# Moving the first GLU pair ahead of three heads of v, the layer norm beside the last pairs, and one low half to DMA

## The chip, the core and the metric

The kernel runs on one core of a Trainium2 chip. The core has TensorE (PE, matrix products; PEld is its weight load), VectorE (DVE), ScalarE (ACT) and GpSimd (POOL), which work side by side, each through its own instructions in order. SyncE (SP) starts most DMA transfers, POOL those that accumulate into their destination. The metric is the time of the program on the device in microseconds: the median of the runs.

## The reference

One layer with two token mixers that share one input projection; x is 1024 tokens by 1024 channels, in float32:

```
h = rmsnorm(x, norm_g)
q, k, v, o, i, f, z_a, glu_in, z_b, ga, gb = split(h @ w_in)
q, k = silu(causal conv of 4 taps over q, k)
hm  = mLSTM(q, k, v, i, f), then RMS norm per head          # 4 heads of 256
y_a = (sigmoid(o) * hm * silu(z_a)) @ w_pa
u   = glu_in[:1024] * sigmoid(glu_in[1024:])
u   = causal conv of 31 taps per channel (u)
u   = silu(layernorm(u) over channels) * silu(z_b)
y_b = u @ w_pb
out = rmsnorm(x + (sigmoid(ga)*y_a + sigmoid(gb)*y_b) @ w_out)
```

## The kernel before, in words

**Products.** Each float32 operand is a high and a low part, and a product is three matmuls (high by high, high by low, low by high). `split` (L102, L103) makes the high part with ScalarE and the low part with VectorE.

**Stages.** First h is made and transposed into `hb`, beside head 0 of v. Then follow three `v_job`s (heads 1 to 3, each of 8 token tiles with 24 matmuls of 128x256; L312 copies four tiles at a time), the mLSTM's gates (`gates`) and `sums`, which forms the sums of blocks of h that Winograd's form of Strassen's scheme needs and keeps them in `ext`. After that come 36 `quad` jobs, called pairs here: each makes two groups of 128 output channels for all tokens out of seven products (X, Z, W banks of PSUM) of twelve 128x512 matmuls. `quad` copies banks with ScalarE (L412, L415, L418), combines with VectorE (L422, L426, L430), and `emit` applies the pair's function. After the pairs come the mLSTM in chunks of 256 tokens together with the projection y_b, then y_a and the output projection.

**Preparation.** `prep(n + 1)` runs beside job n (`run_job`): it splits the weight blocks a11 and a12 (tag "a"), forms the four sums s1 to s4 on VectorE (L198 to L203), splits them (tags "t" and "s") and a22 (tag "b"). For "t" and "s" the low half is a negated copy on ScalarE (L189) to which a DMA of POOL's queue adds the source (L190, `lo…t`, `lo…s`). For "a" and "b" VectorE subtracts (L103). The halves of one pair are `hi…a`, `lo…a` and so on with the job's number.

**Order.** The jobs are gb0 ga0 q0 k0 o0 za0 mb0 ma0, gb1 ga1 and so on, and last zb0 to zb3; numbers 4 to 39. gb and ga are the two sides of the GLU. `glu_job` (ga) leaves two tiles u, and each goes through the 31-tap convolution on VectorE (L498 once, L500 30 times) with a low priority, so that a scheduler places its steps between the other work. There is one accumulator tile `acc`; the finished tile is stored to c_dram by SP and added into s_dram (s1_dram, the sum over channel tiles) by a DMA of POOL (L505). An engine's instructions go in the order that the scheduler set, whatever is ready.

**Layer norm.** `layer_norm` runs beside the last two pairs ahead of zb0: the sum over channels by matmuls with ones (`token_stat`, `tstat`), a transpose (`trow`) and a trip through mu_dram to broadcast it; then eight centred tiles `ct` (`centred`: load, subtract), squared on ScalarE (L585) and added into `sv` by DMAs of POOL (L586); a second statistic, and rstd broadcast into `sv`. `zb_job` loads and centres each tile again, multiplies by `sv` (L599), takes the SiLU (L600), and its pair multiplies SiLU(z_b) by it (L453) and stores to u_dram.

Of the kernel before, what the change touches and what calls it, by code (L numbers as in the profile page):

```python
# [9 lines left out]
F32 = mybir.dt.float32  # L10
# [28 lines left out]
DMA_LOW = True  # L39
# [3 lines left out]
def kernel(ctx: ExitStack, tc: tile.TileContext, x, norm_g, w_in, b_if, conv_qk_w, conv_qk_b,  # L43
# [22 lines left out]
    def ms(name, shape=None):  # L66
# [4 lines left out]
    c_dram, q_dram, k_dram, g_dram, u_dram, oa_dram, sga_dram, sgb_dram, m1_dram = (  # L71
        dram(n, [KT, P, S]) for n in ("c_dram", "q_dram", "k_dram", "g_dram", "u_dram", "oa_dram", "sga_dram", "sgb_dram", "m1_dram"))
# [99 lines left out]
    def prep(n):  # L172
# [28 lines left out]
        s1, s2 = pair("t", sm[0], DMA_LOW)  # L201
# [3 lines left out]
        s3, s4 = pair("s", sm[1], DMA_LOW)  # L205
# [318 lines left out]
    for h in range(H):
        jobs.append(dict(kind="v", h=h, name="v", fn=lambda n, h=h: v_job(n, h)))
    rest = []
    for h in range(H):
        rest.append(("q", lambda n, h=h: qk_job(n, h, 0), Q0, h))
        rest.append(("k", lambda n, h=h: qk_job(n, h, 1), K0, h))
        rest.append(("o", lambda n, h=h: act_job(n, AF.Sigmoid, keep="gate"), O0, h))  # L530
        rest.append(("za", lambda n, h=h: act_job(n, AF.Silu, store=lambda j, h=h: g_dram[2 * h + j],
                                                 by=lambda j: state["gate"][j]), ZA0, h))
        rest.append(("mb", lambda n, i=h: act_job(n, AF.Sigmoid, store=lambda j, i=i: sgb_dram[2 * i + j]), MB0, h))
        rest.append(("ma", lambda n, i=h: act_job(n, AF.Sigmoid, store=lambda j, i=i: sga_dram[2 * i + j]), MA0, h))
    for i in range(4):
        add(f"gb{i}", lambda n: act_job(n, AF.Sigmoid, keep="sg"), GB0_, i)
        add(f"ga{i}", lambda n, i=i: glu_job(n, 2 * i), GA0_, i)
        for name, fn, base, h in rest[6 * i:6 * i + 6]:
            add(f"{name}{h}", fn, base, h)
    first_zb = len(jobs)  # L540
    for i in range(4):
        add(f"zb{i}", lambda n, i=i: zb_job(n, i), ZB0, i)
# [18 lines left out]
    def centred(c, n):  # L561
        ct = state["lnp"].tile([P, S], F32, tag="ct", name=f"ct{n}_{c}", bufs=2)
# [4 lines left out]
    def layer_norm():  # L567

        lnp = state["lnp"]
        mu = lnp.tile([P, S], F32, name="mu")  # L570
        sv = lnp.tile([P, S], F32, name="sv")
        state["mu"], state["rstd"] = mu, sv
        s1 = lnp.tile([P, S], F32, tag="ct", name="s1", bufs=2)
        nc.sync.dma_start(s1, s1_dram)
        ps, st = token_stat(s1, 0)
        nc.vector.tensor_scalar(st, ps, 1.0 / D, None, op0=ALU.mult)
        yield
        to_row(st, 0, mu)
        yield
        for c in range(KT):  # L580
# [6 lines left out]
            yield  # L587
# [462 lines left out]
```

## Time and profile before

| | us |
|---|---|
| runs, median of 3 (range) | 1343.44 (1343.11 to 1345.21) |
| the profiled execution | 1342.88 |
| its span | 1341.1 |
| TensorE busy | 1219.2 |
| VectorE busy | 947.3 |
| ScalarE busy | 624.4 |
| POOL busy | 121.7 |

The profile shows one execution. Its span is from the first instruction to the last; the time of the run has 1.8 us around it. An engine's idle time stands in the row of the instruction that ended it, with what released that instruction. Matmuls are pipelined, so that the starts of successive matmuls are the measure of their pace.

### The profile page before, as it was taken

Reading aid. Unit: us, or ns where it says so; the run is one execution under the profiler, and the core shown is the slowest. Engines: PE = TensorE matmul, PEld = TensorE weight load, DVE = VectorE, ACT = ScalarE, POOL = GpSimd, SP = SyncE. Lnnn points to the kernel's source line nnn. Section 1 sums busy time; section 2 is a strip of 40 time slices with the busy share of each in tenths; the row PEclk is TensorE's granted clock in tenths of the full one; section 3 lists DMA queues with packets and bytes.
Section 4 is the critical chain, followed back from the end, with each engine's and each line's share of the span. In section 5 each row is a group of like instructions: output and inputs, shape, how many; then the busy total and the mean of one; then the engine's idle time right before and its main releaser. Section 6 shows DMA issues by size and latency. Waiting matters only on the chain. (4 is left out here: it accounts for less than half of the span.)

```text
span 1341.1 us, 16597 instructions
## 1 busy us (share of the span) xinstructions
PE 1219.2 (91%) x6204; PEld 1025.1 (76%) x6204; DVE 947.3 (71%) x1250; ACT 624.4 (47%) x916; POOL 121.7 (9%) x229
## 2 busy tenths in 40 slices
PE   8999999999999999989999998255898999899997
PEld 7998878878787787877788786144787887588997
DVE  6882499798998979989798983247886763344433
ACT  6343456544564546644475453236745531222224
POOL 2100100101101010101001011100111110000002
PEclk9999999999999999999999898666899999899999
DMA  7224455766557566576566676748886544453403
GB/s 260 77 64 110 98 138 141 185 145 141 126 141 185 129 142 161 120 190 136 132 173 128 164 168 161 176 129 277 247 263 196 172 155 149 160 171 126 173 17 126
DMA packets 165022, 206.33 MB, mean 154 GB/s; under 512 B 9553, under 2 KB 134857, under 8 KB 164942
## 3 DMA queue, kind: packets, MB, share of 16 engines
q1 hardware_dynamic: 152558, 160.19, 38.1%
q0 software_dynamic: 12384, 45.09, 18.2%
q8 instruction: 48, 0.79, 0.2%
q14 instruction: 32, 0.26, 0.1%
HBM read 113.48 MB, written 50.36 MB: 122 GB/s over the span
## 5 line engine op out<-in xcount | busy, mean ns | idle before, releaser
L500 DVE SCALAR_TENSOR_TENSOR acc<-u,dww,acc 128x1024 f32<-128x1024 f32 x240 | 307.4, 1281 | 3.5
L112 PE MATMUL v<-hi,hb 128*128 128x256 f32 (+1 forms) x512 | 95.2, 289 | 2.5 <-ACT hb L102 2.0
L112 PE MATMUL ya<-oa,whi 128*128 128x512 f32 x256 | 86.4, 414 | 8.5 <-ACT oa L102 4.6
L112 PE MATMUL out<-whi,mrg 128*128 128x256 f32 x512 | 92.3, 283 | 0.0
L112 PE MATMUL yb<-u,whi 128*128 128x512 f32 x256 | 84.7, 407 | 2.0 <-ACT u L102 1.5
L112 PEld LDWEIGHTS v<-hi,hb 128*128 128x128 f32 x512 | 80.0, 192 | 3.6 <-ACT hb L102 2.6
L112 PEld LDWEIGHTS out<-whi,mrg 128*128 128x128 f32 x512 | 79.9, 192 | 0.0
L448 ACT ACTIVATE f<-f 128x512 f32<-128x512 f32 x72 | 45.4, 630 | 67.4 <-DVE f L426 39.8
L112 PE MATMUL out<-wlo,mrg 128*128 128x256 f32 x256 | 72.4, 283 | 0.0
L112 PE MATMUL v<-lo,hb 128*128 128x256 f32 (+1 forms) x256 | 71.7, 289 | 0.0
L112 PEld LDWEIGHTS ya<-oa,whi 128*128 128x128 f32 x256 | 49.2, 194 | 26.7 <-ACT oa L102 7.7
L102 ACT CAST whi<-wr 128x1024 fp32r<-128x1024 f32 x24 | 25.2, 1049 | 76.9 <-PE ya L112 57.4
L470 DVE SCALAR_TENSOR_TENSOR qa<-qr,par,qa 128x1023 f32<-128x1023 f32 (+2 forms) x48 | 59.3, 1277 | 0.0
L112 PEld LDWEIGHTS yb<-u,whi 128*128 128x128 f32 x256 | 46.0, 191 | 10.4 <-ACT u L102 2.5
L112 PE MATMUL ya<-oa,wlo 128*128 128x512 f32 x128 | 52.2, 408 | 0.0
L112 PE MATMUL yb<-u,wlo 128*128 128x512 f32 x128 | 50.8, 397 | 0.0
L112 PEld LDWEIGHTS out<-wlo,mrg 128*128 128x128 f32 x256 | 49.1, 192 | 0.0
L112 PEld LDWEIGHTS v<-lo,hb 128*128 128x128 f32 x256 | 48.4, 193 | 0.0
L202 DVE TENSOR_TENSOR sum<-raw 128x512 f32<-128x512 f32 x36 | 24.8, 689 | 33.2 <-DMA lo4s<-sum 4.3
L564 DVE TENSOR_TENSOR ct<-ct,mu 128x1024 f32<-128x1024 f32 x16 | 19.5, 1223 | 35.2 <-DMA ct<-c_dram 35.0
L957 DVE TENSOR_TENSOR sga<-ya,sga 128x512 f32<-128x512 f32 x16 | 10.3, 686 | 45.9 <-PE ya L112 45.9
L198 DVE TENSOR_TENSOR sum<-raw 128x512 f32<-128x512 f32 x36 | 24.7, 686 | 25.0 <-DMA lo14t<-sum 4.6
(1577 smaller groups left out, 3344.3 us busy)
## 6 DMA issues: line engine op xcount, KB each, us to landing
raw<-in_w_in_dram SPq DMA_DIRECT2D x144, 256.0 KB, 5.1
ct<-c_dram SPq DMA_DIRECT2D x16, 512.0 KB, 5.1
xt<-in_x_dram SPq DMA_DIRECT2D x8, 512.0 KB, 4.0
raw<-in_w_in_dram SPq DMA_DIRECT2D x8, 512.0 KB
v_dram<-vt SPq DMA_DIRECT2D x8, 512.0 KB
q_dram<-qa SPq DMA_DIRECT2D x8, 512.0 KB
k_dram<-qa SPq DMA_DIRECT2D x8, 512.0 KB, 2.7
c_dram<-acc SPq DMA_DIRECT2D x8, 512.0 KB
```

The lines of the kernel that those rows point to most:

```text
L102: ins = nc.scalar.copy(hi, src)
L112: nc.tensor.matmul(ps, a, b, start=(first and j == 0), stop=(last and j == len(todo) - 1))
L198: nc.vector.tensor_tensor(sm[0][:, 0], raw[:, 0], raw[:, 3], op=ALU.add)
L202: nc.vector.tensor_tensor(sm[1][:, 0], raw[:, 0], raw[:, 1], op=ALU.add)
L448: nc.scalar.activation(t[j][:, HF[hf]], src, func, scale=sgn(neg))
L470: nc.vector.scalar_tensor_tensor(acc[j][:, s:], raw[j][:, 0:S - s], cw(KQ - 1 - s, t), acc[j][:, s:], op0=ALU.mult, op1=ALU.add)
L500: nc.vector.scalar_tensor_tensor(acc, u[:, k:k + S], dw(k, c), acc, op0=ALU.mult, op1=ALU.add)
L564: nc.vector.tensor_tensor(ct, ct, state["mu"], op=ALU.subtract)
L957: nc.vector.tensor_tensor(sg[:, sl], ps[:, sl], sg[:, sl], op=ALU.mult)
```

## The change

- gb0 and ga0 run right behind head 0 of v, as "plain" pairs: eight products, block by block, two to a bank, without sums. Their four low halves are all made by VectorE; `emit` takes the banks straight. Then follow v1, v2, v3, with `sums` beside v1 and the end of v3, and then the other 34 pairs in the order of a list, `ORDER`. ga0 to ga3 are jobs 2, 11, 18 and 25.
- zb0 to zb3 only store SiLU(z_b) to z_dram. The last pairs are zb0 zb1 zb2 zb3 o3 za3 mb3 ma3.
- The layer norm runs beside the last six pairs (from job 34, zb2). The squares are added by VectorE. Its second pass has eight steps: load ct and z, centre, multiply, SiLU, multiply, store to u_dram.
- a22's low half is made as those of "t" and "s": a negated copy on ScalarE and a DMA of POOL.
- v1 to v3 use the pairs' four banks, two token tiles in each, copied apart; pools are opened at other places, the sums use the weights' buffers, and the tiles of the mLSTM's chunks lie where the weights' were.

The core of the diff:

```diff
-DMA_LOW = True
+DMA_LOW = "tsb"
+
+ORDER = ("q0 mb0 k0 ma0 gb1 ga1 q1 o0 za0 k1 mb1 gb2 ga2 ma1 q2 o1 za1 k2 gb3 ga3 mb2 q3 o2 za2 k3 ma2 "
+         "zb0 zb1 zb2 zb3 o3 za3 mb3 ma3")
+LN_AT = 28
...
-        def pair(tag, src, dma=False):
+        def pair(tag, src):
             nb = src.shape[1]
             hi, lo = [t[:, 0:nb * 512].rearrange("p (b n) -> p b n", b=nb) for t in halves(n, tag)]
-            if dma:
+            if tag in DMA_LOW and not j["plain"]:
                 nc.scalar.copy(hi, src)
                 nc.scalar.activation(lo, hi.bitcast(F32), AF.Copy, scale=-1.0)
                 nc.gpsimd.dma_start(lo, src, accum_op=ALU.add)
...
+        if j["plain"]:
+            a21, a11 = pair("a", raw[:, 0:2])
+            yield
+            a12, a22 = pair("b", raw[:, 2:4])
+            j["w"] = ((a11, a12), (a21, a22))
+            return
...
-        s1, s2 = pair("t", sm[0], DMA_LOW)
+        s1, s2 = pair("t", sm[0])
...
-            ps = pj(f"v{h}_{g}")
-            psv = ps.rearrange("p (t c) -> p t c", t=4)
+            vt = state["tmp"].tile([P, 4, DH], F32, tag="tmp", name=f"vt{h}_{g}", bufs=5)
             for i in range(4):
                 t = g * 4 + i
-                sl = slice(t * P, (t + 1) * P)
-                mm3(psv[:, i, :], [(hpair(k, sl), wpair(k)) for k in range(KT)])
+                if i % 2 == 0:
+                    ps = state["qb"].tile([P, 2, DH], F32, tag="qb", name=f"v{h}_{t}")
+                mm3(ps[:, i % 2, :], [(hpair(k, slice(t * P, (t + 1) * P)), wpair(k)) for k in range(KT)])
                 yield
-            vt = vt_pool.tile([P, 4, DH], F32, tag="vt", name=f"vt{h}_{g}", bufs=2)
-            nc.scalar.copy(vt, psv)
+                if i % 2:
+                    nc.scalar.copy(vt[:, i - 1:i + 1, :], ps)
...
+        if j["plain"]:
+            for t in range(2):
+                for hf in range(2):
+                    ps = bank(f"c{t}{hf}")
+                    for l in range(2):
+                        product(ps, j["w"][t][l], hb[:, 2 * hf + l], l == 0, l == 1)
+                        yield
+                    emit(t, hf, ps, False)
+            return
...
+        zb=(ZB0, lambda i: lambda n: act_job(n, AF.Silu, store=lambda j: z_dram[2 * i + j])))
...
+    def add_q(name):
+        base, fn = kinds[name[:-1]]
+        i = int(name[-1])
+        add(name, fn(i), base, i, plain=name in ("gb0", "ga0"))
+
+    add_v(0)
+    add_q("gb0")
+    add_q("ga0")
+    for h in range(1, H):
+        add_v(h)
+    for name in ORDER.split():
+        add_q(name)
...
-        s1 = lnp.tile([P, S], F32, tag="ct", name="s1", bufs=2)
+        sv = lns.tile([P, S], F32, name="sv")
+        s1 = state["cv"].tile([P, KD - 1 + S], F32, tag="u", name="s1", bufs=2)[:, 0:S]
...
+        mu = state["cv"].tile([P, S], F32, tag="acc", name="mu", bufs=1)
+        state["mu"] = mu
         to_row(st, 0, mu)
+        yield
...
-                nc.gpsimd.dma_start(sv, ct, accum_op=ALU.add)
+                nc.vector.tensor_tensor(sv, sv, ct, op=ALU.add)
...
-    def zb_job(n, i):
-        cts = []
-        for j in range(2):
-            ct = centred(2 * i + j, 1)
-            nc.vector.tensor_tensor(ct, ct, state["rstd"], op=ALU.mult)
-            nc.scalar.activation(ct, ct, AF.Silu, bias=lb(2 * i + j), scale=lg(2 * i + j))
-            cts.append(ct)
-        return act_job(n, AF.Silu, store=lambda j: u_dram[2 * i + j], by=lambda j: cts[j])
+        for c in range(KT):
+            ct = centred(c, 1)
+            z = state["tmp"].tile([P, S], F32, tag="tmp", name=f"z{c}", bufs=5)
+            nc.sync.dma_start(z, z_dram[c])
+            nc.vector.tensor_tensor(ct, ct, sv, op=ALU.mult)
+            nc.scalar.activation(ct, ct, AF.Silu, bias=lb(c), scale=lg(c))
+            nc.vector.tensor_tensor(z, z, ct, op=ALU.mult)
+            nc.sync.dma_start(u_dram[c], z)
+            yield
...
+    qb_cm, state["qb"] = pool("qb", bufs=4, space=PSUM)
+    lns_cm, lns = pool("lns", reuse_waits="tile")
+    tmp_cm, state["tmp"] = pool("tmp", reuse_waits="tile")
+    cv_cm, state["cv"] = pool("cv", reuse_waits="tile")
...
-    for n in range(4, first_zb - 2):
-        run_job(n)
-    close(cv_cm)
-    ln_cm, state["lnp"] = pool("lnp", reuse_waits="tile")
+    run_job(2)
+    tsums = sums(state["ext"])
+    run_job(3, islice(tsums, 4))
+    run_job(4)
+    run_job(5, chain([0] * 2, tsums))
...
-    for n in range(first_zb - 2, first_zb):
-        run_job(n, ln)
+    for n in range(6, len(jobs)):
+        run_job(n, *([ln] if n >= 6 + LN_AT else []))
...
-    mp_cm, mp = pool("mp", side="right", reuse_waits="tile")
+    u2_cm, u2p = pool("u2p", side="right", reuse_waits="tile")
+    mp_cms, (mpt, mpm, mpa, mp) = zip(*[pool(n, side="right", reuse_waits="tile") for n in ("mpt", "mpm", "mpa", "mp")])
```

How the order of the instructions changes, at three places.

VectorE, at the end of one convolution and the start of the next, before (`sum` is the preparation's, `f` the output of za, `lo18b` a22's low half; `acc_2735` and `acc_2786` are two tiles in one buffer):

```order
L500 SCALAR_TENSOR_TENSOR acc_2735<-u_2627,dww,acc_2735 128x1024
L453 TENSOR_TENSOR f_0_3231<-f_0_3231,f_0_3103 128x1024
L103 TENSOR_TENSOR lo18b<-raw_3226,hi18b 128x512
L453 TENSOR_TENSOR f_1_3232<-f_1_3232,f_1_3104 128x1024
L199 TENSOR_TENSOR sum_0_3423<-sum_0_3423,raw_3358 128x512
L202 TENSOR_TENSOR sum_1_3424<-raw_3358 128x512
L203 TENSOR_TENSOR sum_1_3424<-sum_0_3423,raw_3358 128x512
L498 TENSOR_SCALAR acc_2786<-u_2629,dww,par 128x1024
```

VectorE now, at the end of ga1's first convolution (`qr` is the output of q2):

```order
L519 SCALAR_TENSOR_TENSOR acc_2457<-u_2349,dww,acc_2457 128x1024
L213 TENSOR_TENSOR sum_1_3013<-sum_0_3012,raw_2945 128x512
L519 SCALAR_TENSOR_TENSOR acc_2457<-u_2349,dww,acc_2457 128x1024 x2
L107 TENSOR_TENSOR lo16a<-raw_2945,hi16a 128x1024
L441 TENSOR_TENSOR qr_0_2950<-w_2995,qr_0_2950 128x512
L517 TENSOR_SCALAR acc_2509<-u_2351,dww,par 128x1024
```

Six operations of the pairs stood between two convolutions, now two.

TensorE about the second statistics of the layer norm, before (`z_6387` and `z_6250` are banks of the last two pairs):

```order
L398 MATMUL z_6387<-hb,lo39t 128x512
L549 MATMUL tstat_5930<-ones,sv 128x2
L549 MATMUL tstat_5930<-ones,sv 128x2 x7
L555 MATMUL trow_5942<-ident,tst_5939 8x128
L398 MATMUL z_6250<-hb,hi38s 128x512
```

TensorE about the second statistics now:

```order
L408 MATMUL z_5931<-hb,lo36s 128x512
L577 MATMUL tstat_6042<-ones,sv 128x2
L577 MATMUL tstat_6042<-ones,sv 128x2 x7
L408 MATMUL x_5930<-ext,hi36b 128x512
```

The second statistics stand in the last but three of the pairs now, ahead of its product by a22; before they stood among the last two.

ScalarE, in the second pass of the layer norm, before (`ct` are its tiles, `f` the pairs' outputs, L415 and L412 bank copies):

```order
L600 ACTIVATE ct_0_5953<-ct_0_5953,par 128x1024
L600 ACTIVATE ct_1_5958<-ct_1_5958,par 128x1024
L415 COPY f_1_6248<-z_6250 128x512
L448 ACTIVATE f_1_6248<-f_1_6248 128x512
L412 COPY f_0_6384<-x_6386 128x512
```

ScalarE in the second pass now (`hi39a`, `hi39t` and `lo39t` are halves of the last pair's weights):

```order
L629 ACTIVATE ct_2_6188<-ct_2_6188,par 128x1024
L106 CAST hi39a<-raw_6258 128x1024
L629 ACTIVATE ct_3_6216<-ct_3_6216,par 128x1024
L431 COPY f_0_6263<-x_6265 128x512
L467 ACT_TABLE_LOAD
L467 ACTIVATE f_0_6263<-f_0_6263 128x512
L434 COPY f_1_6264<-z_6266 128x512
L437 COPY f_0_6263<-x_6265 128x512
L192 CAST hi39t<-sum_0_6332 128x1024
L193 ACTIVATE lo39t<-hi39t 128x1024
L629 ACT_TABLE_LOAD
L629 ACTIVATE ct_4_6246<-ct_4_6246,par 128x1024
```

The layer norm's SiLUs stand ahead of the pairs' bank copies in both; now the pairs' function is another one, and the tables of the two alternate.

## Rows read from the trace of the kernel before

**Rows 1.** The page's first part: engine, busy us (share of the span), instructions.

```profile
PE 1219.2 (91%) x6204; PEld 1025.1 (76%) x6204; DVE 947.3 (71%) x1250; ACT 624.4 (47%) x916; POOL 121.7 (9%) x229
```

**Rows 2.** Windows: from:to, length, each engine's busy us (instructions), clock, DMA share, GB/s.

```profile
162.40:323.80 161.40, 158.25 (x683) 127.52 (x682) 143.15 (x154) 86.45 (x108) 15.90 (x20) 1.00 0.62 151
...
811.00:919.00 108.00, 60.98 (x237) 49.05 (x237) 43.21 (x48) 34.68 (x43) 12.17 (x19) 0.74 0.60 162
919.00:945.00 26.00, 16.61 (x75) 15.11 (x76) 19.09 (x29) 19.19 (x35) 0.17 (x3) 0.57 0.93 296
```

**Rows 3.** TensorE's timeline: start, us, instruction, count, [idle before <- what ended it].

```profile
124.28 0.73 PE L398 MATMUL x<-hb,hi4a 128*128 128x512 f32 x2 [2.21 <-ACT vt L312]
...
149.21 0.63 PE L398 MATMUL x<-ext,hi5t 128*128 128x512 f32 x2
...
168.57 0.63 PE L398 MATMUL x<-ext,hi6t 128*128 128x512 f32 x2
...
811.33 3.57 PE L549 MATMUL tstat<-ones,s 128*128 128x2 f32 x16 [6.53 <-DMA s<-s_dram]
...
849.75 0.79 PE L398 MATMUL z<-hb,lo39t 128*128 128x512 f32 x1 [7.21 <-DMA lo39t<-sum]
...
873.10 3.57 PE L549 MATMUL tstat<-ones,sv 128*128 128x2 f32 x16 [18.84 <-DMA sv<-ct]
...
891.47 1.22 PE L398 MATMUL z<-hb,hi38s 128*128 128x512 f32 x2 [12.41 <-ACT f L415]
...
919.95 0.58 PE L112 MATMUL sc<-qh,kh 128*128 128x256 f32 x1 [7.16 <-ACT kh L102]
```

**Rows 4.** TensorE's waits from 124 to 804: total us, times, longest.

```profile
PE x L398 <- DVE f L426: 15.2, 8, 3.5
```

**Rows 5.** VectorE's groups, 162 to 324: busy, mean ns, idle before by releaser.

```profile
L500 DVE SCALAR_TENSOR_TENSOR acc<-u,dww,acc 128x1024 f32<-128x1024 f32 x60 | 76.8, 1280 | 0.9
...
L198 DVE TENSOR_TENSOR sum<-raw 128x512 f32<-128x512 f32 x9 | 6.2, 686 | 7.7 <-DMA lo14t<-sum 4.6 <-DMA lo6t<-sum 2.6 <-issue 0.5
...
L498 DVE TENSOR_SCALAR acc<-u,dww,par 128x1024 f32<-128x1024 f32 x2 | 1.6, 813 | 2.4 <-DMA s_dram<-acc 2.3
...
L103 DVE TENSOR_TENSOR lo8a<-raw,hi8a 128x1024 fp32r<-128x1024 f32 x1 | 1.2, 1217 | 0.0
...
L103 DVE TENSOR_TENSOR lo8b<-raw,hi8b 128x512 fp32r<-128x512 f32 x1 | 0.7, 685 | 0.0
```

**Rows 6.** VectorE's waits from 162 to 812: total us, times, longest.

```profile
DVE acc L498 <- DMA s_dram<-acc: 14.8, 4, 4.7
```

**Rows 7.** The page's DMA issues: count, KB each, median us to landing.

```profile
ct<-c_dram SPq DMA_DIRECT2D x16, 512.0 KB, 5.1
...
s_dram<-acc POOLq DMA_DIRECT2D x7, 512.0 KB, 8.6
sv<-ct POOLq DMA_DIRECT2D x7, 512.0 KB, 5.5
...
lo4t<-sum POOLq DMA_DIRECT2D x1, 512.0 KB, 4.7
...
lo5s<-sum POOLq DMA_DIRECT2D x1, 512.0 KB, 6.3
```

**Rows 8.** VectorE's timeline in the layer norm, columns as in rows 3.

```profile
824.77 2.35 DVE L564 TENSOR_TENSOR ct<-ct,mu 128x1024 f32<-128x1024 f32 x2
...
858.81 1.23 DVE L564 TENSOR_TENSOR ct<-ct,mu 128x1024 f32<-128x1024 f32 x1 [4.69 <-DMA ct<-c_dram]
864.81 1.23 DVE L564 TENSOR_TENSOR ct<-ct,mu 128x1024 f32<-128x1024 f32 x1 [4.78 <-DMA ct<-c_dram]
...
884.30 2.36 DVE L599 TENSOR_TENSOR ct<-ct,sv 128x1024 f32<-128x1024 f32 x2 [3.79 <-DMA sv<-mu_dram]
```

**Rows 9.** The page's DMA queues: packets, MB, share of 16 engines' span.

```profile
q1 hardware_dynamic: 152558, 160.19, 38.1%
q0 software_dynamic: 12384, 45.09, 18.2%
```

More of the change, by code (lines that the diff above doesn't have):

```diff
@@ L204, in prep @@
         yield
-        s3, s4 = pair("s", sm[1], DMA_LOW)
+        s3, s4 = pair("s", sm[1])
         yield
@@ L516, in glu_job, with add @@
         return quad(n, dst, emit)
-    def add(name, fn, base, i):
+    def add(name, fn, base, i, plain=False):
         n = len(jobs)
-        jobs.append(dict(kind="q", name=name, c=(base + 2 * i * P, base + (2 * i + 1) * P), fn=fn))
-        return n
[L524 to L542, printed above, removed]
+        jobs.append(dict(kind="q", name=name, c=(base + 2 * i * P, base + (2 * i + 1) * P),
+                         plain=plain, fn=fn))
@@ new lines, in add, with add_v @@
+        return n
+    def add_v(h):
+        jobs.append(dict(kind="v", h=h, name="v", fn=lambda n: v_job(n, h)))
+    kinds = dict(
+        q=(Q0, lambda i: lambda n: qk_job(n, i, 0)),
+        k=(K0, lambda i: lambda n: qk_job(n, i, 1)),
+        o=(O0, lambda i: lambda n: act_job(n, AF.Sigmoid, keep="gate")),
+        za=(ZA0, lambda i: lambda n: act_job(n, AF.Silu, store=lambda j: g_dram[2 * i + j],
+                                             by=lambda j: state["gate"][j])),
+        gb=(GB0_, lambda i: lambda n: act_job(n, AF.Sigmoid, keep="sg")),
+        ga=(GA0_, lambda i: lambda n: glu_job(n, 2 * i)),
+        mb=(MB0, lambda i: lambda n: act_job(n, AF.Sigmoid, store=lambda j: sgb_dram[2 * i + j])),
+        ma=(MA0, lambda i: lambda n: act_job(n, AF.Sigmoid, store=lambda j: sga_dram[2 * i + j])),
+        zb=(ZB0, lambda i: lambda n: act_job(n, AF.Silu, store=lambda j: z_dram[2 * i + j])))
@@ L635 @@
     next(gate_steps, None)
-    close(vt_cm)
-    close(ift_cm)
     ext_cm, ext_pool = pool("ext_pool", reuse_waits="tile")
     state["ext"] = ext_pool.tile([P, 3, 2, 4, 512], F32R, name="ext")
-    vt_cm, vt_pool = pool("vt2_pool", reuse_waits="tile")
-    tp_cm, tp = pool("tp", reuse_waits="tile")
-    tsums = sums(tp, state["ext"])
-    run_job(2, islice(tsums, 4))
-    run_job(3, chain([0] * 2, tsums))
-    close(tp_cm)
-    close(vt_cm)
-    close(pj_cm)
-    qb_cm, state["qb"] = pool("qb", bufs=4, space=PSUM)
-    tmp_cm, state["tmp"] = pool("tmp", reuse_waits="tile")
-    cv_cm, state["cv"] = pool("cv", reuse_waits="tile")
-    for n in range(4, first_zb - 2):
-        run_job(n)
-    close(cv_cm)
-    ln_cm, state["lnp"] = pool("lnp", reuse_waits="tile")
+    run_job(2)
[3 more added lines that the diff above has]
+    run_job(5, chain([0] * 2, tsums))
     ln = layer_norm()
-    for n in range(first_zb - 2, first_zb):
-        run_job(n, ln)
+    for n in range(6, len(jobs)):
+        run_job(n, *([ln] if n >= 6 + LN_AT else []))
     for _ in ln:
         pass
-    for n in range(first_zb, len(jobs)):
-        run_job(n)
-    close(ln_cm)
+    close(ext_cm)
+    close(cv_cm)
     close(tmp_cm)
-    close(ext_cm)
+    close(lns_cm)
     close(qb_cm)
@@ L732, in loads @@
         def loads():
-            rb = mp.tile([P, CS], F32, tag="rb", name=f"rb{n}", bufs=2)
+            rb = mpa.tile([P, CS], F32, tag="rb", name=f"rb{n}", bufs=2)
             nc.sync.dma_start(rb, r_dram[h:h + 1, sl].broadcast_to([P, CS]))
-            q, k, v = [mp.tile([P, 2, CS], F32, tag=x, name=f"{x}{n}", bufs=2) for x in "qkv"]
+            q, k, v = [mpa.tile([P, 2, CS], F32, tag=x, name=f"{x}{n}", bufs=2) for x in "qkv"]
             for dst, src in ((q, q_dram), (k, k_dram)):
@@ L742, in prepare @@
             rb, q, k, v = (L[x] for x in ("rb", "q", "k", "v"))
-            qh, ql, kh, kl = [mp.tile([P, 2, CS], F32R, tag=x, name=f"{x}{n}", bufs=2) for x in ("qh", "ql", "kh", "kl")]
+            qh, ql, kh, kl = [mpt.tile([P, 2, CS], F32R, tag=x, name=f"{x}{n}", bufs=2) for x in ("qh", "ql", "kh", "kl")]
             nc.scalar.activation(qh, q, AF.Copy, scale=DH ** -0.5)
@@ L751, in prepare @@
             nc.scalar.activation(dm, dm, AF.Exp)
-            vh, vl = [mp.tile([P, 2, VW], F32R, tag=x, name=f"{x}{n}", bufs=2) for x in ("vh", "vl")]
+            vh, vl = [mpm.tile([P, 2, VW], F32R, tag=x, name=f"{x}{n}", bufs=2) for x in ("vh", "vl")]
             split(vh[:, :, 0:DH], vl[:, :, 0:DH], v)
@@ L764, in scores @@
             nc.vector.tensor_tensor(dm, sc[:, 0:3 * P], dm, op=ALU.mult)
-            ph, pl = [mp.tile([P, 3 * P], F32R, tag=x, name=f"{x}{n}", bufs=2) for x in ("ph", "pl")]
+            ph, pl = [mpm.tile([P, 3 * P], F32R, tag=x, name=f"{x}{n}", bufs=2) for x in ("ph", "pl")]
             split(ph, pl, dm)
@@ L878, in u2_tile @@
     def u2_tile(c):
-        ut = u2p.tile([P, 2, S], F32R, name=f"u2_{c}")
+        ut = u2p.tile([P, 2, S], F32R, tag="u2", name=f"u2_{c}", bufs=KT)
         raw = yp.tile([P, S], F32, tag="st", name=f"ur{c}", bufs=2)
@@ L912 @@
             do_split(0)
-    close(mp_cm)
+    for cm in mp_cms[::-1]:
+        close(cm)
     oa_cm, oap = pool("oap", side="right", reuse_waits="tile")
@@ L941, in run @@
             ahead(i, 1)
-    close(u2_cm)
-    mg_cm, mgp = pool("mgp", reuse_waits="tile")
     mrg = []
@@ L953 @@
         ps = run(proj(i, f"ya{d}", rhs=lambda k, sl: (oa[k][:, 0, sl], oa[k][:, 1, sl])), i)
[L954 removed]
+        mt = u2p.tile([P, 2, S], F32R, tag="u2", name=f"mrg{d}", bufs=KT)
         for hf in range(2):
@@ L1016 @@
     close(r_cm)
-    close(mg_cm)
+    close(u2_cm)
     close(yp_cm)
```

53 lines of the change are left out of this document (25 added, 28 removed).

## The prediction

> **What bounds the kernel now.** I read the page's first part, the windows by stage, TensorE's timeline and then its waits. TensorE is busy 91% of the span and VectorE 71% [rows 1], but these are averages over different stages. In the quarter from 162.4 to 323.8 us (eight pairs, two of the eight convolutions) TensorE is busy 158.25 of 161.40 us and VectorE 143.15; from 811 to 919, where the layer norm stands, TensorE has 60.98 of 108.00, VectorE 43.21, and the clock is granted at 0.74 [rows 2]. So the pairs are bounded by TensorE, with VectorE close behind, and the layer norm by a chain of waits.
>
> TensorE's landmarks [rows 3] make the ledger. The same product starts at 149.21 in one pair and at 168.57 in the next: 19.36 us a pair, 2.766 a product. The pairs begin at 124.28. At 811.33 the first statistics matmul starts after a wait of 6.53, so the idle time begins at 804.80; by then 33 pairs and four products (235) are done, worth 650.0 of 680.5 us. Lost: M = 30.5. The last 17 products end at 919.95 − 7.16 = 912.79: 47.0 of 108.0 us, lost L = 61.0. The wait of 7.16 for the first chunk of the mLSTM is T. So 36 × 19.36 = 697.0, plus 30.5, 61.0 and 7.2, is the 795.7 us from 124.28 to 919.95. In L I see 6.53, 7.21, 18.84 and 12.41 of single waits, and statistics matmuls of 3.57 twice.
>
> **The change part by part.**
>
> *Two plain pairs.* gb0 and ga0 need no Winograd sums, so they can run before v1 to v3; they take eight products each: 16 × 2.766 = 44.3 us. The 2.21 that the first pair waited for a whole-bank copy of v [rows 3] should go, as v's banks are now smaller. I take 42 (40 to 46) in place of two pairs of 38.7: **+3.3**. Their combining adds are gone, and conv 0 and 1 get 70 us of v stages to run beside. The rehoused pools and chunk tiles change no instruction's size; I cost them at nothing, hidden by TensorE's work; if a new neighbour in memory makes a load wait, it costs a few us at the transition (in T's bounds).
>
> *The middle, M.* The 28.6 pairs ahead of the first statistics (to the fourth product of job 34) hold two stretches, ga1 to ga2 and ga2 to ga3, with two convolutions in seven pairs instead of eight. VectorE there: 143.15 [rows 2] less a gate pair (seven adds of 0.686, two low halves of 1.217 and 0.685 [rows 5]: 6.7) and less 0.685 for a22's low half in seven pairs (4.8) is 131.7 against 7 × 19.36 = 135.5 for TensorE. That would fit, but a convolution has one accumulator, which the accumulate into s_dram must have read before the next one starts: 8.6 us from issue to landing [rows 7]. Before, enough other work stood at those boundaries that four waits came to 14.8 in all [rows 6]. In the new order 1.7 to 3.6 us of work stand there, so each start waits about 6: 131.7 + 12 = 143.7, 8.2 more than TensorE, twice: 16. The other 14.6 pairs lose what pairs lost before, 30.5/33.6 = 0.91 each (half of it behind VectorE's combining step [rows 4]): 13. **M = 29**, −1.5; bounds 14 (VectorE catches up) and 63 (rival B).
>
> The Trainium skill's DMA: Bandwidth & Descriptors, section Anatomy of one DMA, fits a software DMA as 2.0 us plus bytes over 436 GB/s: an estimate of 3.2 us for these 512 KB. The row shows 8.6 for the accumulating one, so the row decides. By the page the boundaries would hardly wait, and M would be about 14.
>
> *a22's low half by DMA.* 34 times 0.685 leaves VectorE, and one negating copy on ScalarE and one more DMA in POOL's queue come in, behind t's, s's and in places behind s_dram's. Such DMAs land in 4.7 to 6.3 us [rows 7]; the half is used by the pair's last product, and the preparation runs a pair ahead, so 16 us cover it. Zero in the sum; not below zero beyond VectorE's relief, counted above; the upper end is rival D.
>
> *Layer norm, L.* First pass: TensorE has 16 products (44.3 us) between the two statistics in the new order. The chain between is 13.4 us from the first statistics to the first centred tile (811.33 to 824.77 [rows 3, 8]), then eight tiles. Before they came every 6.0 us, with VectorE waiting 4.7 for each load [rows 8]; two buffers, and a square summed on VectorE (1.22) in place of the 5.5 us accumulate [rows 7], give about 4.5: 36. Together 49.4, 5 over; with weights on the same queues up to 13. I take 7. The statistics and their transposes themselves: 8. Second pass: 61 us of products are left, and the chain is 11.2 of statistics and broadcast (873.10 to 884.30 [rows 3, 8]) plus eight tiles of about 7.2 (a load of 5.1 [rows 7] and four operations of 1.22, two deep, with stores standing between them on SP): 69, 8 over. ScalarE also has silus and table loads ahead of the bank copies, of the kind that gave TensorE 12.41 in before [rows 3]: 6. The ordinary 0.91 for these 5.4 pairs: 5. **L = 8 + 7 + 14 + 5 = 34**, −27; bounds 20 and 61.
>
> The same page (section Issuing engines are not separate DMA queues) says that DMAs of all issuing engines end on the same 16 and interleave. That speaks against this change; it stands beside rival C, and no row of before has these transfers at once. By rows: hardware transfers took 38.1% of 1341.1 us for 160.19 MB, 3.19 us of all engines a MB, software ones 5.41 [rows 9]. The first pass moves about 9 and 2.5 MB in its 44.3 us, 42 us of all engines; the second, with z's load and u's store, about 15.5 and 3.6 MB in 61 us, 69. Both are as long as their chains, which is why I take L's bounds so wide.
>
> *Transition and behind it.* T stays 7.2: the chunk loads still follow the last stores on SP. From 919 to 945 TensorE is busy 16.61 of 26.00 at 0.57 of the clock, with the last pair's centring, silus and stores beside the first chunks and DMA at 0.93 [rows 2]. These are gone: **−6** (0 to −9, of 9.4 idle).
>
> **Sum.** 42 + 34 × 19.36 (658.2) + 29 + 34 + 7.2 = 770.4 in place of 795.7: −25.3, and −6: −31.3. The profiled execution took 1342.88 (1341.1 of span and 1.8 around it), 0.6 under the median of 1343.44, so the same step off the median gives 1312.
>
> **The rivals.**
> B, VectorE becomes the bound of all pairs from ga1 to zb1 (22). For it: it is busy 89% there now, and its waits, for low halves above all (4.6 at one sum of the quarter [rows 5]), stay. 22 pairs would need 7.6 each (131.7 less two convolutions of 0.81 + 30 × 1.280 [rows 5], by seven), six convolutions (235), 2.3 of idle each (18.25 in eight now [rows 2]) and five accumulator waits (30): 483 against 426, and 0.91 for the other six: M = 63, 1346. With half of those idle times it is 38. Against it: a late VectorE finds the low halves landed.
> C, the layer norm isn't hidden: its waits are handed to TensorE by ScalarE's and VectorE's in-order queues, as 12.41 was. L stays 61: 1339 with M as above, and no change at all with an M of 33 or more. It decides if a tile of the second pass takes some 11 us.
> D, slower: a22's low half comes late. POOL's queue is in order, an accumulate of 8.6 stands ahead, and TensorE did once wait 7.21 for a low half [rows 3]. From 0.9 us a pair (31 over 34) the gain is gone; at 2 us it is 68: 1380. Against it: one such wait in 36 pairs of before.
> E, the accumulator waits are taken up by slack and the first pass hides: M = 14, L = 24: 1287.
>
> **How the numbers follow.** My forecast, 1312 (its own range 1298 to 1325), has 0.48; the ground between it and B, half-way B and C alone in it, 0.22; E 0.14; B itself, or C with half of B, at no change, 0.06; D, or B with C on top, 0.10. A range of 1289 to 1341 takes in the first two and most of E. Faster by over 0.2% (about what a measurement of this kernel can tell from no change): 0.84, within: 0.06, slower: 0.10.
>
> **What would show it.** In the changed profile: the first Winograd pair at about 166 us; the first statistics matmul 28.6 pairs later with M read off as above; VectorE's waits for s_dram<-acc of about 30 in all, near six starts; TensorE's waits at the second statistics (sv) under 10; no wait of TensorE for lo…b; the granted clock from ga1 to the last pair near 1. I am wrong if TensorE waits for lo…b, if the pairs run 21 us or more on average (B), or if TensorE's idle time beside zb2 to ma3 is over 30 (C).

## The result, and the profile after

The changed kernel takes 1313.65 us (median of four runs, 1311.6 to 1314.68) beside 1343.28 for the kernel before. The ratio is 0.9777, with a 95% interval from 0.9763 to 0.9792: 29.6 us or 2.2% faster. The forecast was 1312. The profiled execution took 1314.68, with a span of 1312.9.

The windows of the changed kernel, cut at its landmarks (columns as in [rows 2]): from the first Winograd pair to the first statistics, from there to the second, from there to the last pair's end, and the first 70 us of the mLSTM.

```profile
162.88:747.71 584.83, 564.59 (x2403) 452.69 (x2401) 489.93 (x508) 324.77 (x414) 82.49 (x98) 0.99 0.69 164
747.71:801.33 53.62, 48.74 (x211) 38.59 (x209) 31.13 (x36) 29.26 (x38) 5.21 (x6) 0.97 0.83 224
801.33:888.06 86.73, 70.17 (x282) 54.94 (x280) 45.60 (x50) 50.66 (x60) 9.45 (x10) 0.90 0.79 237
895.97:965.97 70.00, 58.23 (x342) 50.76 (x343) 56.41 (x120) 46.80 (x98) 9.96 (x30) 0.90 0.83 256
```

Before, the layer norm's 108 us had TensorE busy for 60.98 at a clock of 0.74 [rows 2]. Now the two middle rows together, which hold 38 products in place of 17, have it busy for 118.91 of 140.35, at 0.97 and 0.90.

TensorE's timeline at the same landmarks (start, us, instruction, idle time before and what ended it):

```profile
162.88 0.63 PE L408 MATMUL x<-hb,hi6a 128*128 128x512 f32 x2
...
747.71 1.85 PE L577 MATMUL tstat<-ones,s 128*128 128x2 f32 x16
...
801.33 1.84 PE L577 MATMUL tstat<-ones,sv 128*128 128x2 f32 x16
...
806.97 1.22 PE L408 MATMUL x<-ext,hi36b 128*128 128x512 f32 x2 [3.80 <-DVE f L445]
...
847.71 0.80 PE L408 MATMUL x<-hb,lo39a 128*128 128x512 f32 x1 [5.92 <-DVE lo39a L107]
...
872.22 0.75 PE L408 MATMUL x<-ext,hi39t 128*128 128x512 f32 x2 [3.21 <-ACT f L431]
...
895.97 0.58 PE L116 MATMUL sc<-qh,kh 128*128 128x256 f32 x1 [7.91 <-ACT kh L106]
```

Neither statistics waits any more, where before they waited 6.53 and 18.84 [rows 3]. From these rows the ledger is read as the prediction did, with 2.766 us a product: 200 products lie between the first pair's start and the first statistics, 38 between these and 895.97 − 7.91 = 888.06, where the last pair ends.

| term | before | forecast | after |
|---|---|---|---|
| first pair's start, against 124.28 | 0 | +42 | +38.6 |
| pairs at 19.36 | 697.0 | 658.2 | 658.2 |
| M, lost to the first statistics | 30.5 | 29 | 31.6 |
| L, lost from there to the last pair's end | 61.0 | 34 | 35.2 |
| T, wait for the first chunk | 7.2 | 7.2 | 7.9 |
| from the first chunk to the end (span − sc) | 421.1 | 415.1 | 416.9 |

The loss that is gone is L's: 25.8 us. The later start and the two pairs fewer cancel (38.6 against 38.8), and the other terms move by five or less.

VectorE's waits for the accumulator (total, times, longest), from 100 to 820 us:

```profile
DVE acc L517 <- DMA s_dram<-acc: 17.1, 5, 7.1
```

This answers to [rows 6]: 14.8 before. TensorE's waits nowhere name a low half of a22; its largest groups of waits from 165 to 775 us are for VectorE's combining step and, once, a bank copy:

```profile
PE x L408 <- DVE qr L445: 11.7, 5, 5.1
PE x L408 <- DVE f L445: 5.3, 4, 2.4
PE x L408 <- ACT f L431: 3.5, 1, 3.5
```

### The profile page after: what moved, and what is told of

The parts are those of the page before. It is cut to its first block, busy times and chain, and to the rows that moved or that the text cites. A ratio compares the mean times of both kernels' runs of the same rounds, so it can differ in the third digit from the quotient of the medians.

```text
span 1312.9 us, 16737 instructions
## 1 busy us (share of the span) xinstructions
PE 1219.8 (93%) x6228; PEld 1019.6 (78%) x6228; DVE 929.5 (71%) x1207; ACT 638.6 (49%) x948; POOL 142.0 (11%) x252
## 5 line engine op out<-in xcount | busy, mean ns | idle before, releaser
L467 ACT ACTIVATE f<-f 128x512 f32<-128x512 f32 x69 | 43.1, 630 | 39.3 <-DVE f L445 24.3
L212 DVE TENSOR_TENSOR sum<-raw 128x512 f32<-128x512 f32 x34 | 23.4, 689 | 34.7 <-ACT f L437 6.9
L208 DVE TENSOR_TENSOR sum<-raw 128x512 f32<-128x512 f32 x34 | 23.4, 689 | 24.9 <-ACT lo10b L193 3.5
L1023 ACT ACTIVATE junk<-res 128x256 f32<-128x256 f32 x32 | 13.4, 418 | 48.9 <-DVE res L1022 42.4
```

Of the source, the lines that this page charges most:

```text
L208: nc.vector.tensor_tensor(sm[0][:, 0], raw[:, 0], raw[:, 3], op=ALU.add)
L212: nc.vector.tensor_tensor(sm[1][:, 0], raw[:, 0], raw[:, 1], op=ALU.add)
L467: nc.scalar.activation(t[j][:, HF[hf]], src, func, scale=sgn(neg))
L1023: nc.scalar.activation(junk, r, AF.Square, accum_out=ss[:, t, n:n + 1])
```

## The experiments

Theory 1 is the prediction's: the gain is the layer norm's chain under cover of six pairs (L); VectorE bounds the stretches with two convolutions in seven pairs (M); the plain pairs pay by the cover that they give two convolutions. Its rivals: other queues and engines set these times, so that the part in question costs or gives nothing. Theory 2, formed behind the first eight runs, is that the layer norm costs TensorE some 30 us wherever it stands, by the order in which its operations wait in the queues, and that the addition of the squares on VectorE is a large part of the gain.

Each time is compared by its ratio to the kernel before on the same chip (there at 1341.1 to 1341.8); 0.9777 is the changed kernel's. A point of the ratio is 13.4 us. Where the loss of a stage is given, it is read from one profile as in the table above. The stretch behind the first chunk has the same work wherever the layer norm stands beside the changed kernel's pairs; it varied from 407.7 to 417.2 over these runs, and nothing here shows why. So a stage's loss and the whole time can differ by some us.

### One part undone: a22's low half

```diff
-DMA_LOW = "tsb"
+DMA_LOW = "ts"
```

> The changed kernel with a22's low half subtracted by VectorE again. Theory 1 (VectorE bounds the two stretches of seven pairs with two convolutions): VectorE gets 34 times 0.6 us back, some 4.3 in each stretch and a little elsewhere, so 1320 to 1326. Rival (POOL's queue or the DMA engines are the limit there): 1310 to 1314.

Measured: 1309.31, ratio 0.9766 (0.9725 to 0.9806). By the time the rival's range is the nearer: this part of the change is worth nothing that can be told within the interval (5 us either way). The rival's cause, a limit by POOL's queue or the DMA engines, isn't shown by that. The windows of this run, first pair to first statistics and on to the last pair's end, say where the expected loss went:

```profile
163.22:753.11 589.89, 563.29 (x2402) 450.60 (x2400) 507.99 (x538) 311.56 (x385) 56.51 (x69) 0.99 0.61 148
753.11:891.99 138.88, 120.85 (x490) 94.78 (x490) 78.20 (x88) 79.28 (x94) 10.37 (x11) 0.91 0.79 239
```

VectorE has 18.1 us more than in the changed kernel, and M is 36.7, 5.1 more, which is theory 1's direction; but L is 1.4 less, T 2.2 and the stretch behind it 5.6 less.

### One part undone: the plain pairs

```diff
-    add_v(0)
-    add_q("gb0")
-    add_q("ga0")
-    for h in range(1, H):
+    for h in range(H):
         add_v(h)
-    for name in ORDER.split():
+    for name in ("gb0 ga0 " + ORDER).split():
...
-        add(name, fn(i), base, i, plain=name in ("gb0", "ga0"))
+        add(name, fn(i), base, i, plain=False)
...
-    run_job(2)
-    tsums = sums(state["ext"])
-    run_job(3, islice(tsums, 4))
+    tsums = sums(state["ext"])
+    run_job(2, islice(tsums, 4))
+    run_job(3, chain([0] * 2, tsums))
     run_job(4)
-    run_job(5, chain([0] * 2, tsums))
+    run_job(5)
```

> The changed kernel with gb0 and ga0 behind v3 again and with Winograd's seven products; the rest as changed. Theory 1 (the plain pairs pay by giving convolutions 0 and 1 the v stages as cover): 5.6 us fewer products, 5.4 us of idle time back in the v stages, and some 15 to 20 us of VectorE's excess from ga0 to ga1, so 1325 to 1335. Rival (they are a price paid for nothing): 1305 to 1310.

Measured: 1326.4, ratio 0.9867 (0.9829 to 0.9905), 0.9 points more than the changed kernel, or 12 us. Theory 1's range holds. The windows, pairs to the first statistics and on to the last pair's end:

```profile
119.77:766.08 646.31, 611.21 (x2571) 488.14 (x2570) 546.25 (x563) 343.74 (x439) 87.24 (x105) 0.97 0.66 158
766.08:906.37 140.29, 118.70 (x491) 93.10 (x489) 76.71 (x84) 79.87 (x97) 14.66 (x16) 0.93 0.80 232
```

The first pair starts at 119.77, 4.5 earlier than before the change. So the stages ahead of it became shorter without plain pairs too, and theory 1 had that wrong: TensorE's waits there (from 40 us on) come to 2.0, where they were 5.7. So the plain pairs cost 162.88 − 119.77 = 43.1 us of start for 38.7 of Winograd pairs, 4.4. M is 646.31 − 214 × 2.766 = 54.4, 22.8 more. L is 35.2, the same as with them. The plain pairs buy 22.8 us of M for 4.4. That is 18.4; the time shows 12, as the stretch behind the first chunk is 8.0 shorter in this run.

### The layer norm taken away

The statistics and both passes are left out; zb0 to zb3 store SiLU(z_b) as u.

```diff
-        zb=(ZB0, lambda i: lambda n: act_job(n, AF.Silu, store=lambda j: z_dram[2 * i + j])))
+        zb=(ZB0, lambda i: lambda n: act_job(n, AF.Silu, store=lambda j: u_dram[2 * i + j])))
...
-        run_job(n, *([ln] if n >= 6 + LN_AT else []))
+        run_job(n)
...
```

> The changed kernel without the layer norm: zb0 to zb3 store SiLU(z_b) as u, the statistics and both passes are left out. Theory 1 (of the 35 us that TensorE loses from the first statistics to the last pair's end some 30 are the layer norm's, handed over by in-order queues): 1279 to 1288. Rival (the last pairs lose them to their own banks and low halves): 1300 or more.

Measured: 1278.82, ratio 0.9521 (0.9499 to 0.9542), 34 us under the changed kernel. All of the pairs:

```profile
163.55:854.58 691.03, 669.33 (x2858) 539.21 (x2856) 521.92 (x549) 380.19 (x488) 95.41 (x113) 0.99 0.67 160
```

691.03 − 658.2 = 32.8 is lost in all 34 pairs together, 1.2 more than M alone in the changed kernel. The 201st product, with which L began above, starts here:

```profile
749.26 0.63 PE L408 MATMUL x<-ext,hi34s 128*128 128x512 f32 x2
```

From there to 854.58 the 38 products lose 105.3 − 105.1 = 0.2. So the last pairs lose nearly nothing of their own, and the 35.2 of L are the layer norm's: theory 1 holds.

### Two accumulators

```diff
-            acc = cv.tile([P, S], F32, tag="acc", name=f"acc{c}", bufs=1)
+            acc = cv.tile([P, S], F32, tag="acc", name=f"acc{c}", bufs=2)
...
-        sv = lns.tile([P, S], F32, name="sv")
...
-        mu = state["cv"].tile([P, S], F32, tag="acc", name="mu", bufs=1)
+        mu = state["cv"].tile([P, S], F32, tag="acc", name="mu", bufs=2)
...
+        sv = state["cv"].tile([P, S], F32, tag="acc", name="sv", bufs=2)
```

> The changed kernel with two accumulator tiles for the convolutions (mu and sv take them in the layer norm). Theory 1 (a convolution's start waits for the accumulate into s_dram, and VectorE bounds those stretches): the 17 us of such waits are gone and 6 to 12 of them come off, 1302 to 1308. Rival (VectorE waits for something else then): 1312 to 1314.

Measured: 1291.69, ratio 0.9622 (0.9599 to 0.9645), 1.55 points or 21 us under the changed kernel: more than theory 1 expected.

```profile
163.01:730.23 567.22, 557.59 (x2403) 449.24 (x2402) 482.33 (x506) 324.42 (x414) 82.26 (x99) 1.00 0.72 173
730.23:870.04 139.81, 118.68 (x491) 93.23 (x489) 75.57 (x83) 79.83 (x97) 14.66 (x16) 0.93 0.78 228
```

M falls from 31.6 to 14.0, by 17.6. The waits for s_dram<-acc, 17.1 us, are gone from VectorE's list. L is 34.7, nearly unchanged. T and the stretch behind it are 6.0 shorter.

The same edit in the kernel before (its `acc` alone):

> The kernel before with two accumulator tiles and nothing else. Theory 1 (there VectorE has slack, 143 of 161 us in eight pairs, so its 14.8 us of accumulator waits were mostly taken up): 1 to 7 us off, 1335 to 1341. Rival (they cost TensorE one for one there too): 1327 to 1331.

Measured: 1319.38, ratio 0.9843 (0.9814 to 0.9871): 21 us off, beyond the rival. TensorE's timeline at the first statistics, and its waits from 124 to 784:

```profile
790.55 3.57 PE L549 MATMUL tstat<-ones,s 128*128 128x2 f32 x16 [6.85 <-DMA s<-s_dram]
```

```profile
PE x L398 <- DVE f L426: 6.3, 7, 1.3
PE x L398 <- ACT vt L312: 2.2, 1, 2.2
```

The first pair starts there at 124.59, so M = 790.55 − 6.85 − 124.59 − 650.0 = 9.1, after 30.5. A second accumulator takes away most of what TensorE lost in the pairs before, though VectorE was busy only 143.15 of 161.40 us there. The waits of [rows 6] come to 14.8, and 21.4 came off.

But the edit does more than end the waits. With one tile, the second convolution of a GLU pair starts when the first is done. With two, the scheduler's order lets both run side by side, and with it the order of VectorE's other operations changes. VectorE's timelines show the start of the second convolution in the kernel before and in this run, where the first one began at 166.29:

```profile
255.58 0.81 DVE L498 TENSOR_SCALAR acc<-u,dww,par 128x1024 f32<-128x1024 f32 x1 [2.32 <-DMA s_dram<-acc]
```

```profile
171.82 0.81 DVE L498 TENSOR_SCALAR acc<-u,dww,par 128x1024 f32<-128x1024 f32 x1
```

The changed kernel's order moves in the same way: the convolutions of ga2 start at 433.94 and 505.96 with one tile, at 418.17 and 420.69 with two. So the gain of both runs is the second tile's. How much of it is the wait and how much the new order was not taken apart.

### The layer norm at other places

```diff
-LN_AT = 28
+LN_AT = 31
```

> The changed kernel with the layer norm begun beside job 37 and not 34. Theory 1 (the gain is that the layer norm's chain of some 150 us has 38 products beside it): 58 us less of cover, part of it found beside the first chunks, so 1328 to 1348. Rival (its cost is what its operations take on the engines, wherever they stand): 1310 to 1318.

Measured: 1313.75, ratio 0.9796 (0.9767 to 0.9825). Theory 1 falls. The stretch from the first statistics to the last pair's end, the first 70 us of the mLSTM, and TensorE's first matmul in them:

```profile
807.24:862.33 55.09, 52.14 (x239) 41.57 (x237) 32.58 (x36) 31.75 (x41) 8.24 (x11) 1.00 0.74 221
875.64:945.64 70.00, 48.73 (x251) 42.76 (x251) 60.74 (x108) 52.17 (x91) 6.36 (x24) 0.74 0.82 275
```

```profile
875.64 0.58 PE L116 MATMUL sc<-qh,kh 128*128 128x256 f32 x1 [13.31 <-ACT kh L106]
```

The first statistics stand here with 17 products left, as in the kernel before. L is 8.1, 27.1 less than in the changed kernel; but TensorE waits 13.31 for the first chunk in place of 7.91, is busy 48.73 of the next 70 us where the changed kernel has 58.23, and from the first chunk to the end 434.2 pass, 17.3 more. Beside the first chunks the second pass costs nearly as much as beside the pairs.

With two accumulators, one pair earlier (`LN_AT = 27`) and three later (`LN_AT = 31`):

> The changed kernel with two accumulators and the layer norm begun one pair earlier. With two accumulators the last convolution is done some 17 us earlier than before. Theory 2 (the layer norm costs TensorE some 30 us by queues in order wherever it stands): as with two accumulators alone, 1288 to 1294. Rival (more cover helps): 1280 to 1287.

> The changed kernel with two accumulators and the layer norm begun beside job 37. Theory 2: as with one accumulator, the wait moves from the pairs to the first chunks, 1288 to 1296. Rival (with the chain left uncovered more is lost once the pairs are quicker): 1298 or more.

Measured: 1292.54, ratio 0.9634 (0.9609 to 0.9659), and 1293.88, ratio 0.9648 (0.9628 to 0.9667). Both agree with two accumulators alone at 0.9622 within their intervals: theory 2's first half holds, that the cost is much the same at each of these places. That it comes by the order in the queues is read from rows like those below, and no run changed that order alone.

### The squares

In the changed kernel undone, and alone in the kernel before:

```diff
-                nc.vector.tensor_tensor(sv, sv, ct, op=ALU.add)
+                nc.gpsimd.dma_start(sv, ct, accum_op=ALU.add)
```

> The changed kernel with the squares added into sv by POOL's accumulating DMAs, as before the change. Theory 1 (the first pass is a chain that is already longer than its 16 products): seven tiles come at 6.0 us instead of some 4.9, so 8 us more, 1318 to 1326. Rival (first pass covered): 1311 to 1315.

Measured: 1324.18, ratio 0.986 (0.9827 to 0.9893), 0.8 points or 11 us over the changed kernel. Theory 1 holds here. The second statistics of this run:

```profile
820.86 2.13 PE L577 MATMUL tstat<-ones,sv 128*128 128x2 f32 x16 [3.32 <-DMA sv<-ct]
```

The first ones start at 748.45, so 72.4 us lie between the two, 53.6 with VectorE's additions. L is 48.9 against 35.2.

> The kernel before with one edit: the squares are added into sv by VectorE. Theory 2 (a good third of the change's gain is this line: undone, it cost the changed kernel 11 us): the wait of 18.84 before the second statistics shrinks by 8 to 14, so 1328 to 1334. Rival (before, the loads of ct set the pace of 6.0 us a tile, and the accumulate only follows them): 1338 to 1341.

Measured: 1323.44, ratio 0.987 (0.9851 to 0.9889). This one line makes the kernel before 17 us faster, and theory 2 had it too small. TensorE's timeline:

```profile
812.96 3.58 PE L549 MATMUL tstat<-ones,s 128*128 128x2 f32 x16 [6.96 <-DMA s<-s_dram]
...
855.44 3.57 PE L549 MATMUL tstat<-ones,sv 128*128 128x2 f32 x16 [6.72 <-DVE sv L586]
...
873.86 1.22 PE L398 MATMUL z<-hb,hi38s 128*128 128x512 f32 x2 [12.46 <-ACT f L415]
```

The wait of 18.84 is 6.72, and 42.5 us lie between the statistics in place of 61.8. L is 896.23 − 806.00 − 47.0 = 43.2. VectorE's timeline of the centred tiles (columns as in [rows 8]):

```profile
840.90 1.23 DVE L564 TENSOR_TENSOR ct<-ct,mu 128x1024 f32<-128x1024 f32 x1 [0.35 <-DMA ct<-c_dram]
843.72 1.23 DVE L564 TENSOR_TENSOR ct<-ct,mu 128x1024 f32<-128x1024 f32 x1 [1.60 <-DMA ct<-c_dram]
844.86 2.55 DVE L586 TENSOR_TENSOR sv<-sv,ct 128x1024 f32<-128x1024 f32 x2
849.36 1.23 DVE L564 TENSOR_TENSOR ct<-ct,mu 128x1024 f32<-128x1024 f32 x1 [1.95 <-DMA ct<-c_dram]
851.70 1.23 DVE L564 TENSOR_TENSOR ct<-ct,mu 128x1024 f32<-128x1024 f32 x1 [1.11 <-DMA ct<-c_dram]
```

The tiles come every 4.2 us (840.90 to 849.36, two apart), where they came every 6.0 with waits of 4.7 for the load [rows 8]. The loads were as long as before (5.2 at the median, 5.1 before), so what had been late was their start. The waits of SP, which starts the loads of ct (L563), name the cause, before and in this run:

```profile
SPq L563 <- DMA sv<-ct: 43.0, 7, 7.7
```

```profile
SPq L563 <- DVE sv L586: 23.7, 7, 6.3
```

A load into a tile stood behind the accumulate that still read it, 43.0 us in all; behind VectorE's addition it is 23.7.

### SiLU pairs last

mb3 and ma3 take the places of q3 and k3 in `ORDER`, and these come last.

```diff
-ORDER = ("q0 mb0 k0 ma0 gb1 ga1 q1 o0 za0 k1 mb1 gb2 ga2 ma1 q2 o1 za1 k2 gb3 ga3 mb2 q3 o2 za2 k3 ma2 "
-         "zb0 zb1 zb2 zb3 o3 za3 mb3 ma3")
+ORDER = ("q0 mb0 k0 ma0 gb1 ga1 q1 o0 za0 k1 mb1 gb2 ga2 ma1 q2 o1 za1 k2 gb3 ga3 mb2 mb3 o2 za2 ma3 ma2 "
+         "zb0 zb1 zb2 zb3 o3 za3 q3 k3")
```

> The changed kernel with mb3 and ma3 in the places of q3 and k3 and these as the last two pairs, so that the pairs beside the layer norm's second pass use the same table as its SiLUs. Theory 1 (table loads of 1.28 us on ScalarE stand ahead of the pairs' bank copies): six to eight fewer, 3 to 8 us off, 1305 to 1310. Rival (TensorE waits there for loads and stores, through VectorE's and ScalarE's order): 1311 to 1316; with the convolutions of q3 and k3 ahead of the first chunk, slower.

Measured: 1319.88, ratio 0.9836 (0.9788 to 0.9883): some 8 us slower than the changed kernel, with intervals that just overlap. Theory 1's gain didn't come, though its table loads went: from 747 us to the last pair's end ScalarE has two, where the changed kernel has nine. TensorE has one wait of 13 in the last pair:

```profile
883.67 1.22 PE L408 MATMUL x<-ext,hi39t 128*128 128x512 f32 x2 [13.01 <-ACT qr L431]
```

and ScalarE's timeline shows what stood ahead of that bank copy:

```profile
874.78 1.24 ACT L487 ACTIVATE qa<-qr,par 128x1024 f32<-128x1024 f32 x1 [2.68 <-DMA u_dram<-z]
877.29 1.24 ACT L487 ACTIVATE qa<-qr,par 128x1024 f32<-128x1024 f32 x1 [1.27 <-DMA u_dram<-z]
880.90 1.24 ACT L629 ACTIVATE ct<-ct,par 128x1024 f32<-128x1024 f32 x1 [2.37 <-DVE ct L628]
882.09 1.06 ACT L491 ACTIVATE qa<-qa 128x1024 f32<-128x1024 f32 x1
883.05 0.57 ACT L431 COPY qr<-x 128x512 f32<-128x512 f32 x1
```

ScalarE has no table load in these rows, but waits for the stores of u (which free the tiles) and for VectorE. So fewer table loads did not pay by enough to be seen; what they cost by themselves isn't shown, since with the pairs exchanged the convolutions of q3 and k3 (L487) stand there too.

### u's stores by POOL, with two accumulators

```diff
-            nc.sync.dma_start(u_dram[c], z)
+            nc.gpsimd.dma_start(u_dram[c], z)
```

> The changed kernel with two accumulators and u's stores in POOL's queue, so that they no longer stand between the loads of ct on SP. Theory 2 (TensorE's loss in the second pass is loads that come late through SP's order): 1281 to 1288. Rival (the late loads come of the two tiles for ct, and the low halves now stand behind the stores): 1290 to 1298.

Measured: 1287.85, ratio 0.9599 (0.9575 to 0.9623). It is the fastest of all these kernels, but its interval overlaps that of two accumulators alone (0.9599 to 0.9645), so that the stores' queue isn't settled as a cause.

```profile
729.24:866.64 137.40, 117.01 (x491) 91.77 (x489) 75.84 (x83) 79.29 (x97) 19.21 (x24) 0.93 0.80 232
```

L is 32.3 in that profile, 2.4 less than with two accumulators alone, and most of the rest of the 7.0 us between the two spans lies at the first pair's start (0.9) and behind the first chunk (3.8).

## Why the prediction was right, and where not

**The start.** 42 was forecast, 38.6 came. The price of the plain pairs was right (44.3 by products, 43.1 measured), but the stages ahead of the first pair are 4.5 shorter, twice the 2.21 that I credited to the banks. That the pairs give two convolutions the v stages as cover stood in the prediction without a number; undone, it was 22.8 us of M. It is the largest thing that I didn't price.

**M.** 29 forecast, 31.6 measured, by a sum whose terms were off, so that the nearness is partly luck. I expected some 30 us of accumulator waits at six starts, of which 16 would reach TensorE; there were 17.1 at five (in the two dense stretches the four starts waited 7.1, 1.3, 4.6 and 0.2, 13.2 in place of 24), and M fell by 17.6 with a second tile. That is the term's size, but not its proof, as the second tile changed VectorE's order too. The "ordinary" 0.91 a pair was wrong as a kind: in the kernel before, a second tile took 21.4 of the 30.5 us away, and 0.27 a pair is what is left (9.1 over 33.6). What stands in that term's place is 14.0 of loss in 28.6 pairs for which no single cause was shown. The Trainium skill's fit (DMA: Bandwidth & Descriptors, section Anatomy of one DMA), an estimate of 3.2 us for such a DMA, lies under the rows: the accumulates of the changed kernel landed in 5.8 at the median, with waits of up to 7.1 behind them.

**a22's low half.** I set it to zero with VectorE's relief counted in M (4.8 in each dense stretch). M is 5.1 lower with it than without, but the time is not; rival D's waits never came.

**L.** 34 forecast, 35.2 measured: 53.62 − 44.3 = 9.4 to the second statistics and 86.73 − 60.9 = 25.9 behind it, where the sum, with the statistics and the ordinary loss shared out, had 13 and 21. One was too high and the other too low, so that the sum's nearness is luck in part. Two things in it were wrong. I took the gain for cover, six pairs beside the chain. The run with the layer norm three pairs later had only 17 products beside it and was as fast; so the place decides nothing between these. And the addition on VectorE, which I had as one of several reasons for a shorter first pass, is more than half of it: alone, in the kernel before, it takes L from 61.0 to 43.2. The five us of ordinary loss in L don't exist (0.2 in the 38 products without a layer norm).

What remains of L is rival C's mechanism at a smaller price. TensorE's waits come to 21.3 us there, under the 30 that were to speak for C. Behind the second statistics they are 16.4: 3.80 for a combining step, 0.91 and 5.92 for the high and the low half of the last pair's weights, 3.21 and 2.58 for bank copies. The rest of L is the statistics' own matmuls and products at the lower clock of these stretches (0.97 and 0.90). The four long waits are for operations that stand behind the layer norm's on VectorE or ScalarE. VectorE's timeline in the changed kernel shows one:

```profile
805.09 1.23 DVE L592 TENSOR_TENSOR ct<-ct,mu 128x1024 f32<-128x1024 f32 x1 [3.51 <-DMA ct<-c_dram]
806.23 0.68 DVE L445 SCALAR_TENSOR_TENSOR f<-x,f 128x512 f32<-128x512 f32 x1
```

The combining step waits behind a tile's load, and TensorE's matmul at 806.97 behind that, 3.80. The low half that TensorE waited 5.92 for stands in the same way behind a centring at 842.09, which waited 3.06 for its load.

**The transition.** T was forecast unchanged and is 7.9; behind it 4.2 came off, not 6. As that stretch varied by 9.5 between runs, neither figure is confirmed by it.

The parts in the time, each undone or done alone: the plain pairs 12 us, the squares 11 (17 in the kernel before), a22's low half none, the layer norm's place none. If they add up, they come to 23 of 29.6; the rest is shared among parts that were not taken apart, the finer banks of v with the 4.5 of start among them. Another is that zb0 to zb3 no longer wait for the second pass, which no run undid. Two runs bear on it: with 17 products behind the first statistics and the squares on VectorE in both, from the end of the product ahead of these statistics to the end of the program 514.4 us pass in the kernel before with that one line (1320.4 − 806.00), and 502.6 in the changed kernel with the layer norm three pairs later (1309.8 − 807.24). The 11.8 between them hold the free second pass, but also the other order of the pairs and the mLSTM's tiles.

## What to carry to other kernels

A loss that is spread thinly over many steps may still have one remedy: a second accumulator tile took 21 us off either kernel, where the rows of waits showed 14.8 and 17.1. Before calling a rate per step ordinary, take away the one wait that the other engine's list names; and look at what else the edit moved, for a second tile also changed the order. A DMA that reads a tile held the tile's next load back here; where the engine has time, adding there can be worth more than the engine's time it costs. And a chain moved under other work still takes the engines' order with it: ask which waits it carries into the queues there.

## What the runs showed of the hardware

The same 16 matmuls of one statistic took 3.57 us behind an idle time of 6.53 [rows 3], and 1.85 and 1.84 where TensorE had not waited (747.71 and 801.33 above). The windows of the first statistics, before and after, show the clock that was granted in them, 0.50 and 1.00, the lower and the higher of the two levels (1.2 and 2.4 GHz):

```profile
811.33:814.90 3.57, 3.57 (x17) 3.57 (x17) 0.00 (x0) 0.00 (x0) 0.00 (x0) 0.50 0.99 211
```

```profile
747.71:749.40 1.69, 1.69 (x17) 1.69 (x16) 1.69 (x3) 1.01 (x1) 0.00 (x0) 1.00 0.25 32
```

So that wait cost its own length and 1.7 us more in the 16 matmuls behind it.

An accumulate of 512 KB into s_dram landed in 8.6 us at the median before [rows 7], and in 5.8 in the changed kernel, though the DMA engines' share beside the pairs was higher there (0.69 against 0.62). What shortened it wasn't tried.
